# Writing out TensorE's order for the second mixer of a two-block transformer kernel

## The chip, the cores and the metric

The kernel runs on one core of a Trainium2 chip. The metric is the device time of one execution in microseconds (us). The profile is of one execution and its span is counted from the first instruction to the last. TensorE is PE in the profile (PEld is its weight load), VectorE is DVE, ScalarE is ACT, GpSimd is POOL, and SP is the queue that issues most DMAs.

## The reference, cut to what matters

Two blocks run one after the other on 512 tokens of width 1024: a first block (feed-forward, a mixer of three attention branches, feed-forward) and a second block. In the second block a mixer precedes a convolved feed-forward layer. Only the second mixer is changed. It computes:

```
h = rms_norm(x, pre_mix_norm);  proj = h @ w_in            # 1024 -> 6688 columns
q, k, v = split(silu(causal_dwconv(q|k|v)))                # delta rule: 8 heads of 128
o_a = gdn_chunked(l2(q)/sqrt(128), l2(k), v, g, beta)      # scan over chunks, one triangular solve each
o_a = rms_norm(o_a, gdn_norm_w) * silu(z_a)
x_s, b, c = split(silu(causal_dwconv(x_s|b|c)))            # state space: 16 heads of 64, 2 groups
y = (ssd_chunked(x_s, dt, a, b, c) + d * x_s) * silu(z_s)
o_s = rms_norm(y, per group)
x = x + rms_norm(concat(o_a, o_s) @ w_out, post_mix_norm)
```

## The kernel before, in words

Activations lie with features on the partitions and the 512 tokens along the free axis. A large product is made in **steps**: one step multiplies a 128x128 tile of weights with a 128x512 tile of activations as three matmuls (`mm3`, lines 163 to 169), since weights and activations are split in a high and a low half. `wload` (line 146) fetches 4 x 256 columns of weights (512 KB, two buffers) by SP and makes the two halves: ACT casts the high one (line 157), VectorE, or POOL where `k.lo` is set, subtracts for the low one (line 158). One such load serves 8 steps. `gemm_steps` (line 179) is a generator that yields after each step and calls `evac` when a 128-column result is complete; `gemm_fm` runs it to its end. The results of a group of 256 columns use two of three PSUM banks (tag g); small matmuls and transposes use tags a (1 bank), b (3) and r (1).

`Mix2.run` (line 1794) calls the parts in order: `gates` (line 1369: step sizes, decays and their cumulative sums); `gdn_k` and `gdn_a` for both halves of the heads (convolved keys, their transposes, norms, and the tables A = k k^T times decay, line 1504); `gdn_qv`, `blocks32` (line 1538: POOL inverts the 32x32 diagonal blocks of all tables, between DMAs through DRAM), `gdn_qe`, `gdn_qk` (scores); `inverses` (line 1574: the blocks are joined to the inverses of 128x128 tables); `gdn_scan` (line 1615: a serial chain over four chunks); `gdn_norm` (line 1656, with the turning back of the outputs, line 1672); `ssd_gemms`, `ssd` (line 1704), `gdn_z`, `ssd_z` (gates), `ssd_norm`; the product with w_out over 16 tiles, `os` and `oa`, of which `oa` (the delta rule) comes first in the sum; and the closing norm, whose factor is spread over partitions by TensorE and multiplied in before the feed-forward layer.

`conv_silu` (line 1289) evacuates a product with conv: a VectorE product (line 1293), an ACT scaling (1294), three VectorE multiply-adds (1296) and the ACT silu (1298 or 1300). `turned` (line 1337) makes four transposes into one bank. `row` (line 1344) broadcasts a row of decays by one matmul into bank r.

The order of each engine's instructions comes from the framework's scheduler, which goes by the order of the program as priority and by its own model of times. Two things steer it: `high_priority` around the weight halves, and `after=` (line 161), which ties the start of a product behind a matmul of the scans. Only the first mixer has TensorE's order written by hand (line 848, `manual_schedule`): there TensorE runs its instructions in the order of the program text, while the other engines are scheduled as everywhere.

Of the kernel before, what the change touches and what calls it, by code (L numbers as in the profile page):

```python
# [4 lines left out]

# [22 lines left out]
class K:  # L28
# [150 lines left out]
    def gemm_steps(self, w, c0, ncols, x, evac, kmax=4, after=None):  # L179

        nk = len(x)
# [1093 lines left out]
class Mix2:  # L1275
# [25 lines left out]

    def ztile(self):

        return self.k.sp.tile([128, 2, 512], F32, name=self.k.uid("zs"), tag="zs", bufs=2)
# [39 lines left out]
    def row(self, i=None, pick=None):  # L1344


        ps = self.k.ps("row", "r")
# [21 lines left out]
    def gates(self):  # L1369
# [7 lines left out]
        self.rt = k.norm_of(k.row_sums(k.sumsq(self.h)), D)  # L1377
        self.R = k.spread(self.rt)
        f = k.tmp("smf")
        nc.scalar.copy(f[:32], ps[:32])  # L1380
        pt = k.ps("smt")
# [14 lines left out]
        k.load_consts("cums")  # L1396
        pc = k.ps("pc")
# [29 lines left out]
        pt = k.ps("prow")  # L1427
# [5 lines left out]
        nc.vector.tensor_copy(self.pick, k.c("pick"))  # L1433

# [4 lines left out]
    def gdn_k(self, hf):  # L1439
        k, nc, a = self.k, self.nc, self.a  # L1440
        self.st[hf] = {"k": []}
# [7 lines left out]
        k.gemm_fm(a["w_in_2"][0], 1024 + hf * 512, 512, self.y, ev_k)  # L1449

    def gdn_qv(self, hf):
        k, nc, a = self.k, self.nc, self.a
        win = a["w_in_2"][0]
        st = self.st[hf]
        st["q"], st["v"] = qt, vb = self.big("q"), self.big("vb")

        def ev_q(m, ps):
            self.gconv(hf * 4 + m, ps, qt[:, m])

        def ev_v(m, ps):  # L1460
            t = k.tmp("vf", tag="f")
            self.gconv(16 + hf * 4 + m, ps, t)
            pt = self.turned(t, "a")
            for b in range(NB):
                nc.scalar.activation(vb[:, m, b * 128:(b + 1) * 128], pt[:, b * 128:(b + 1) * 128], AF.Copy,
                                     scale=self.vscale[:, b, hf * 4 + m:hf * 4 + m + 1])

        k.gemm_fm(win, hf * 512, 512, self.y, ev_q)
        k.gemm_fm(win, 2048 + hf * 512, 512, self.y, ev_v)

    def gdn_a(self, hf):
        k, nc = self.k, self.nc
        st = self.st[hf]
        ks = st["k"]

        (x, xv), (r, rv), (t, tv), (_, b2) = (self.per_head("kn" + c) for c in "xrtb")
        st["kd"] = []
        for m in range(4):

            pt, kd = self.turned(ks[m], "b"), k.tmp("kd", tag="kd")  # L1480
            self.sums_turned(xv[:, :, m:m + 1], pt)
            for b in range(NB):
                s = slice(b * 128, (b + 1) * 128)
                nc.scalar.activation(kd[:, s], pt[:, s], AF.Copy, scale=self.dec[:, b, hf * 4 + m:hf * 4 + m + 1])
            st["kd"].append(kd)
# [8 lines left out]
        for m in range(4):  # L1494
            hh = hf * 4 + m
# [3 lines left out]
            nc.scalar.activation(d1, d1, AF.Exp, scale=-1.0)  # L1499
            pkk = k.ps("pkk", "b")  # L1500
            for b in range(NB):
# [3 lines left out]
                                               op0=ALU.mult, op1=ALU.mult)  # L1505

    def gdn_qe(self, hf):

        k, nc = self.k, self.nc
        st = self.st[hf]  # L1510
        qt = st["q"]
        st["qe"] = qe = self.per_head("qe")[0]
        x, xv = self.per_head("qx")
        for m in range(4):
            self.sums_turned(xv[:, :, m:m + 1], self.turned(qt[:, m], "b"))
        nc.vector.tensor_scalar(qe, x, EPS, 128.0 * EPS, op0=ALU.add, op1=ALU.mult)

    def gdn_qk(self, hf):
        k, nc = self.k, self.nc
        st = self.st[hf]  # L1520
# [502 lines left out]
```

## Time and profile before

| | before |
|---|---|
| three runs, us | 2233.55, 2235.99, 2236.47 (median 2235.99) |
| profiled execution, us | 2238.18 (span 2236.5) |
| TensorE busy | 2173.7 us, 97% |
| VectorE, ACT, POOL busy | 1255.2 (56%), 933.8 (42%), 325.1 us (15%) |
| DMA | 202.39 MB, mean 90 GB/s |
| mean granted TensorE clock | 0.991 |

The second mixer runs from about 1308 to 1856 us of the span, the first from about 415 to 943. In the table of 40 slices each slice is 55.9 us; a digit 9 is nine tenths or more. Busy times of matmuls overlap, since they are pipelined: what one costs is read from the distance of starts, not from its own duration. A group of instructions has its idle time beside it, with what ended that time.

### The profile page before, as it was taken

The numbers are of one execution on the slowest core, as the hardware profiler recorded it, in microseconds if no ns is written. First come the engines' busy times: TensorE is split into PE (matmuls) and PEld (weight loads), VectorE is DVE, ScalarE is ACT, GpSimd is POOL, SyncE is SP. The second block draws the span as 40 slices with busy tenths as digits, with TensorE's granted clock in tenths as the row PEclk, the third lists the DMA queues.
The fourth block names the chain that finished last, engine by engine and source line by source line (L and its number), as shares of the span: only waits on it lengthen the run. The fifth ranks groups of instructions, "written<-read, shape, count | busy, mean of one in ns | idle before, by whom it ended". The sixth has DMA issues, their size and how long they took to land. (4 is left out here: it accounts for less than half of the span.)

```text
span 2236.5 us, 27895 instructions
## 1 busy us (share of the span) xinstructions
PE 2173.7 (97%) x10700; PEld 1759.4 (79%) x10700; DVE 1255.2 (56%) x2155; ACT 933.8 (42%) x1537; POOL 325.1 (15%) x340
## 2 busy tenths in 40 slices
PE   8999999999999999999999999999999898999998
PEld 6788888777677777788888877878777787888887
DVE  4544433575699654544343347866677526777623
ACT  4333322355555444332322237554556525444421
POOL 0110100011122222011110021550312100000000
PEclk9999999999999999999999999999999998999999
DMA  4233333322222223333333332331122223333332
GB/s 152 86 113 104 95 109 113 94 67 69 69 85 72 66 76 95 113 89 102 95 95 108 113 88 76 86 111 39 56 67 57 76 94 113 95 96 103 95 94 94
DMA packets 198508, 202.39 MB, mean 90 GB/s; under 512 B 19556, under 2 KB 184063, under 8 KB 198375
## 3 DMA queue, kind: packets, MB, share of 16 engines
q1 hardware_dynamic: 197607, 198.12, 29.8%
q0 software_dynamic: 768, 2.49, 0.4%
q8 instruction: 84, 1.38, 0.3%
q14 instruction: 49, 0.40, 0.1%
HBM read 192.70 MB, written 7.88 MB: 90 GB/s over the span
## 5 line engine op out<-in xcount | busy, mean ns | idle before, releaser
L163 PE MATMUL pg<-yh,whi 128*128 128x512 f32 x1856 | 745.6, 402 | 5.9 <-ACT yh L225 2.3
L169 PE MATMUL pg<-yh,wlo 128*128 128x512 f32 x1856 | 730.2, 394 | 1.2 <-DVE wlo L158 1.1
L168 PE MATMUL pg<-yl,whi 128*128 128x512 f32 x1856 | 729.7, 393 | 0.0
L158 DVE TENSOR_TENSOR wlo<-raw,whi 128x1024 fp32r<-128x1024 f32 x341 | 423.7, 1243 | 517.7 <-ACT whi L157 513.7
L157 ACT CAST whi<-raw 128x1024 fp32r<-128x1024 f32 x349 | 362.1, 1038 | 633.2 <-PE pg L168 429.7
L163 PEld LDWEIGHTS pg<-yh,whi 128*128 128x128 f32 x1856 | 350.3, 189 | 81.7 <-issue 9.1
L169 PEld LDWEIGHTS pg<-yh,wlo 128*128 128x128 f32 x1856 | 349.9, 189 | 75.4 <-DVE wlo L158 2.9
L168 PEld LDWEIGHTS pg<-yl,whi 128*128 128x128 f32 x1856 | 350.3, 189 | 67.5 <-issue 2.5
L163 PE MATMUL pg<-hidh,whi 128*128 128x512 f32 x352 | 138.7, 394 | 0.0
L169 PE MATMUL pg<-hidh,wlo 128*128 128x512 f32 x352 | 138.0, 392 | 0.0
L168 PE MATMUL pg<-hidl,whi 128*128 128x512 f32 x352 | 136.6, 388 | 0.0
L361 POOL TENSOR_TENSOR hp<-ut,sg 128x512 f32<-128x512 f32 x44 | 73.3, 1667 | 424.1 <-DVE ut L359 399.5
L217 ACT CAST hidh<-hp 128x512 fp32r<-128x512 f32 x44 | 27.3, 620 | 142.5 <-POOL hp L361 142.3
L169 PEld LDWEIGHTS pg<-hidh,wlo 128*128 128x128 f32 x352 | 66.1, 188 | 15.5
L1910 DVE SCALAR_TENSOR_TENSOR fo<-ft,fcw,fo 128x511 f32<-128x511 f32 x88 | 65.8, 749 | 21.7 <-ACT fo L1907 20.5
L168 PEld LDWEIGHTS pg<-hidl,whi 128*128 128x128 f32 x352 | 66.1, 188 | 14.8
L163 PEld LDWEIGHTS pg<-hidh,whi 128*128 128x128 f32 x352 | 66.2, 188 | 13.1
L218 DVE TENSOR_TENSOR hidl<-hp,hidh 128x512 fp32r<-128x512 f32 x44 | 30.4, 691 | 79.6 <-ACT hidh L217 79.6
L715 POOL TENSOR_SCALAR s<-s,den 128x256 f32<-128x256 f32 (+3 forms) x80 | 42.5, 533 | 190.6 <-DVE den L714 180.0
L1951 PE MATMUL pd<-whi,hidh 128*128 128x512 f32 x176 | 69.4, 394 | 0.0
L1952 PE MATMUL pd<-whi,hidl 128*128 128x512 f32 x176 | 69.4, 394 | 0.0
L1953 PE MATMUL pd<-wlo,hidh 128*128 128x512 f32 x176 | 69.2, 396 | 0.0
(502 smaller groups left out, 3000.1 us busy)
## 6 DMA issues: line engine op xcount, KB each, us to landing
raw<-in_w_in SPq DMA_DIRECT2D x100, 512.0 KB
raw<-in_ffn_w_gate SPq DMA_DIRECT2D x40, 512.0 KB
raw<-in_ffn_w_up SPq DMA_DIRECT2D x40, 512.0 KB
raw<-in_ffn_w_down SPq DMA_DIRECT2D x40, 512.0 KB
raw<-in_w_up SPq DMA_DIRECT2D x40, 512.0 KB
raw<-in_w_out SPq DMA_DIRECT2D x24, 512.0 KB
raw<-in_w_down SPq DMA_DIRECT2D x22, 512.0 KB
raw<-in_w_branch SPq DMA_DIRECT2D x12, 512.0 KB
```

Source lines behind the costliest of these rows:

```text
L157: nc.scalar.copy(hi, raw)
L158: (self.lo or nc.vector).tensor_sub(lo, raw, hi.bitcast(F32))
L163: first = mm(out, whi, xhi, start=start, stop=False)
L168: mm(out, whi, xlo, start=False, stop=False)
L169: mm(out, wlo, xhi, start=False, stop=stop)
L218: nc.vector.tensor_sub(lo, x, hi.bitcast(F32))
L361: nc.gpsimd.tensor_mul(p, ut, sg[m])
L715: nc.gpsimd.tensor_scalar(p[:, :w], p[:, :w], den, 1.0, op0=ALU.mult, op1=ALU.mult)
L1910: nc.vector.scalar_tensor_tensor(o[:, s:], t[:, :T - s], k.fcw[:, j:j + 1], o[:, s:], op0=ALU.mult, op1=ALU.add)
L1951: nc.tensor.matmul(pss[b], xh[:, s], hi[:, i], start=st, stop=False)
L1952: nc.tensor.matmul(pss[b], xl[:, s], hi[:, i], start=False, stop=False)
L1953: nc.tensor.matmul(pss[b], xh[:, s], lo[:, i], start=False, stop=sp)
```

## The change

TensorE's order in the second mixer is written out by hand. A generator `products()` makes the 544 product steps of the mixer one after the other; `fill(n)` takes n of them, and `later(n, do)` puts small work behind the n-th step from now. Because a conv's result is handed over in the call of its last step, `later(10, ...)` leaves 9 steps between (k), 11 leaves 10 (q) and 9 leaves 8 (v and x).

- The parts become generators that yield where product steps go. `gates` stops at steps 3, 6, 13 and 24; the inverses of both halves begin at step 184 with one step between sections; each scan has 3, 3 and 1 steps between its hand-offs, and its outputs (p3) come behind the state update (p4). The eight outputs of the delta rule are turned from 16 steps (first half) and 26 steps (second half) behind the second scan; the state-space groups begin at step 298; the last state-space gate ends at step 416; each state-space norm is summed 8 and spread 11 calls after its last gate.
- Keys are transposed one by one behind their conv (`gdn_kt`), tables follow in pairs of `decay` and `table`, `blocks32` follows the last table.
- `row` uses banks r and a in turn. POOL makes the low weight halves in `gdn_z(0)` and `ssd_gemms(0)` too (12 loads), beside those of the keys as before. `load_consts("cums")` moves ahead of the products.
- The order of the sum of w_out is kept, but tiles are exchanged: the outputs of the delta rule are split into the slots that the state-space outputs had, ahead of step 416, and those of the state space into the slots of the normed input.
- While the closing norm is computed, TensorE makes 7 and 8 matmuls of 128x512 whose results are not used.

The core of the diff:

```
+    def later(self, n, do):
+        at = self.done + n
+        i = sum(d[0] <= at for d in self.due)
+        self.due.insert(i, (at, do))
...
     def row(self, i=None, pick=None):
-        ps = self.k.ps("row", "r")
+        self.nrow += 1
+        ps = self.k.ps("row", "ra"[self.nrow % 2])
...
+    def idle(self, n, a, b):
+        k = self.k
+        ps = k.ps("idle", "r")
+        for _ in range(n):
+            self.nc.tensor.matmul(ps, a[0][:, :128], b[0], start=True, stop=True)
...
         def ev_v(m, ps):
             t = k.tmp("vf", tag="f")
             self.gconv(16 + hf * 4 + m, ps, t)
-            pt = self.turned(t, "a")
+            self.later(9, lambda: turn(m, t))
...
+        def products():
+            k.lo = nc.gpsimd
+            yield from self.gdn_k(0)
+            yield from self.gdn_k(1)
+            k.lo = None
+            yield from self.gdn_q(0)
+            yield from self.gdn_v(0)
+            yield from self.gdn_q(1)
+            yield from self.gdn_v(1)
+            k.lo = nc.gpsimd
+            yield from self.gdn_z(0)
+            yield from self.ssd_gemms(0)
+            k.lo = None
+            yield from self.ssd_gemms(1)
+            yield from self.gdn_z(1)
+            yield from self.ssd_z()
+            yield from k.gemm_steps(a["w_out_2"][0], 0, D, self.out, ev, nk=16)
...
+        def fill(n):
+            for _ in range(n):
+                next(work, None)
+                self.done += 1
+                while self.due and self.due[0][0] <= self.done:
+                    self.due.pop(0)[1]()
...
+        with self.tc.manual_schedule(engines={mybir.EngineType.PE}):
+            gates = self.gates()
+            next(gates)
+            for n in (3, 6, 13, 24):
+                upto(n)
+                next(gates)
+            upto(184)
+            both = [self.inverses(hf) for hf in range(2)]
+            for _ in range(7):
+                for steps in both:
+                    next(steps, None)
+                    fill(1)
+            woven(self.gdn_scan(0))
+            for m in range(4):
+                self.gdn_qk(1, m, 5 * m)
+            fill(19)
+            woven(self.gdn_scan(1))
+            for hf in range(2):
+                self.gdn_norm(hf)
+                for m in range(4):
+                    self.later(16 + 10 * hf + 2 * m, partial(self.gdn_out, hf, m))
+            upto(298)
+            group = self.ssd()
+            for g in range(2):
+                woven(group(g))
...
+            self.out += [k.split(self.st[hf]["q"][:, m], "oa", slot) for hf in range(2) for m in range(4)]
+            upto(416)
+            self.out += [k.split(x, "os", k.yslot) for x in self.xs[:4]]
+            upto(544)
+            idle = lambda n: self.idle(n, self.out[0], self.out[8])
+            sums = k.row_sums(sq)
+            idle(7)
+            pb = k.spread(k.norm_of(sums, D), copy=False)
+            idle(8)
```

## Rows read from the trace of the kernel before

**Rows 1.** Stretches: start:end, length, busy us (instructions) by engine, granted clock, DMA

```profile
core 0: us, PE busy (x) PEld busy (x) DVE busy (x) ACT busy (x) POOL busy (x), PEclk, DMA share, GB/s
1308.00:1856.00 548.00, 522.44 (x2998) 420.69 (x2998) 361.17 (x626) 289.32 (x534) 140.46 (x138) 0.98 0.27 79
425.00:890.00 465.00, 453.41 (x2353) 356.07 (x2352) 315.67 (x793) 236.92 (x462) 94.56 (x138) 0.99 0.25 74
1478.70:1482.10 3.40, 3.40 (x11) 2.71 (x10) 1.25 (x3) 2.51 (x6) 2.16 (x3) 0.50 0.52 189
1768.10:1772.30 4.20, 4.17 (x10) 3.30 (x11) 1.23 (x1) 1.04 (x1) 0.00 (x0) 0.50 0.00 0
1855.80:1861.00 5.20, 5.20 (x12) 4.09 (x13) 5.20 (x9) 3.43 (x6) 0.00 (x0) 0.50 0.59 189
...
1788.00:1828.00 40.00, 40.00 (x177) 32.85 (x176) 11.42 (x11) 12.41 (x16) 0.00 (x0) 1.00 0.29 93
```

**Rows 2.** TensorE's waits, 1308 to 1856 us: total us, times, longest

```profile
PE pg L168 <- DVE oal L218: 4.7, 1, 4.7
PE pb L321 <- POOL ry L244: 3.8, 4, 1.7
PE tr L1341 <- POOL q L1670: 3.2, 5, 1.5
PE tr L1341 <- ACT vf L1298: 2.6, 2, 2.4
PE pg L163 <- ACT yh L225: 2.3, 1, 2.3
PE tr L1341 <- ACT kf L1298: 1.9, 1, 1.9
PE pc L1400 <- DMA ct<-in_consts: 1.6, 1, 1.6
PE pkk L1503 <- DVE A L1504: 1.3, 1, 1.3
PE prow L1429 <- DVE parts L1426: 1.0, 1, 1.0
```

**Rows 3.** Order of time, two convs (k, then v): first and last operation of each

```profile
1341.29 0.69 DVE L1293 TENSOR_TENSOR cx<-pg,R 128x512 f32<-128x512 f32 x1 [2.90 <-PE pg L169]
...
1349.27 0.63 ACT L1298 ACTIVATE kf<-kf 128x512 f32<-128x512 f32 x1
...
1414.12 0.69 DVE L1293 TENSOR_TENSOR cx<-pg,R 128x512 f32<-128x512 f32 x1
...
1419.62 0.63 ACT L1298 ACTIVATE vf<-vf 128x512 f32<-128x512 f32 x1 [1.79 <-DVE vf L1296]
```

**Rows 4.** Order of time, behind the second scan: last copy, first four POOL products

```profile
1582.45 0.57 ACT L1654 COPY q<-sc 128x512 f32<-128x512 f32 x1
...
1590.51 5.61 POOL L1670 TENSOR_TENSOR q<-q,onr 128x512 f32<-128x512 f32 x4 [27.56 <-ACT whi L157]
```

**Rows 5.** Order of time, gates: the small transposes and the log decays

```profile
1318.46 0.43 PE L1383 MATMUL smt<-ct_base,smf 32*128 32x32 f32 x4
...
1328.39 0.25 DVE L1394 TENSOR_TENSOR g<-dt,nega 128x96 f32<-128x96 f32 x1
```

**Rows 6.** Order of time: last table, last write-backs of the blocks, a turned tile

```profile
1405.48 0.35 DVE L1504 SCALAR_TENSOR_TENSOR A<-pkk,knb,d 128x128 f32<-128x128 f32 x1
...
1480.78 3.13 POOL L1569 DMA_DIRECT2D A<-xtscr  x4 [0.39 <-DMA xtscr<-zs]
...
1491.36 0.60 PE L1341 MATMUL tr<-ct_base,vf 128*128 128x128 f32 x4
```

**Rows 7.** A stretch in the first state-space group (columns as in rows 1)

```profile
1628.00:1668.00 40.00, 39.56 (x190) 30.12 (x188) 31.34 (x47) 22.00 (x30) 4.51 (x4) 1.00 0.23 67
```

**Rows 8.** POOL's weight splits, one VectorE operation beside one, its shape elsewhere

```profile
L158 POOL TENSOR_TENSOR wlo<-raw,whi 128x1024 fp32r<-128x1024 f32 x8 | 19.7, 2467 | 31.2 <-ACT whi L157 31.1
...
1331.31 2.26 DVE L1296 SCALAR_TENSOR_TENSOR kf<-cx,gcw,kf 128x509 f32<-128x509 f32 x1
...
L1296 DVE SCALAR_TENSOR_TENSOR bc<-cx,scw,bc 128x509 f32<-128x509 f32 x4 | 3.0, 744 | 0.0
```

More of the change, by code (lines that the diff above doesn't have):

```diff
@@ L4 @@
 from contextlib import ExitStack
+from functools import partial
 import numpy as np
@@ L1447, in ev_k, with gdn_kt @@
             ks.append(t)
[L1449 to L1462, printed above, removed]
-            pt = self.turned(t, "a")
[L1464 to L1471, printed above, removed]
+            self.later(10, lambda: self.gdn_kt(hf, m))
+        yield from k.gemm_steps(a["w_in_2"][0], 1024 + hf * 512, 512, self.y, ev_k)
+    def gdn_kt(self, hf, m):
         k, nc = self.k, self.nc
         st = self.st[hf]
[L1474 to L1485, printed above, removed]
+        (x, xv), (r, rv), (t, tv), (_, b2) = st["n"]
+        pt, kd = self.turned(st["k"][m], "b"), k.tmp("kd", tag="kd")
+        self.sums_turned(xv[:, :, m:m + 1], pt)
+        for b in range(NB):
+            s = slice(b * 128, (b + 1) * 128)
+            nc.scalar.activation(kd[:, s], pt[:, s], AF.Copy, scale=self.dec[:, b, hf * 4 + m:hf * 4 + m + 1])
+        st["kd"].append(kd)
+        if m < 3:
+            return
         nc.vector.tensor_scalar(x, x, EPS, None, op0=ALU.add)
@@ L1690, in ev_x, with turn @@
             self.conv_silu(ps, *cols(m), t)
+            self.later(9, lambda: turn(m, t))
+        def turn(m, t):
             pt = self.turned(t, "a")
@@ L1707, in ssd, with group @@
         free = self.slots()
-        for g in range(2):
+        def group(g):
             bm, cm = self.bc[g], self.bc[2 + g]
@@ L1719, in ssd @@
             bt = next(free)
+            yield 1
             nc.scalar.copy(bt, self.turned(bm, "b"))
@@ new lines, in table @@
+            def table(c, p):
+                L = k.tmp("L")
+                self.decay_t(L, 8 + 2 * (g * 4 + c) + p)
+                nc.vector.tensor_mul(L, L, cb)
+                return L
+            ls = []
+            for c in range(5):
+                new = []
+                for p in range(2):
+                    if c < 4:
+                        new.append(table(c, p))
+                        yield 2
+                if c:
+                    m = g * 4 + c - 1
+                    pd = k.ps("pyd", "b")
+                    for p, L in enumerate(ls):
+                        for b in range(NB):
+                            nc.tensor.matmul(pd[p * 64:(p + 1) * 64, blk[b]],
+                                             self.xdt[g][:, c - 1, b * 128 + p * 64:b * 128 + p * 64 + 64], L[:, blk[b]],
+                                             start=True, stop=True)
+                    po = k.ps("pyo", "b")
+                    for b in range(1, NB):
+                        nc.tensor.matmul(po[:, blk[b]], states[b][:, (c - 1) * 128:c * 128], cm[:, blk[b]],
+                                         start=True, stop=True)
+                    er = self.row(pick=pick[:, (c - 1) * 128:c * 128])
+                    x = self.xs[m]
+                    nc.vector.tensor_add(x, x, pd)
+                    t = k.tmp("yo")
+                    nc.scalar.copy(t[:, 128:], po[:, 128:])
+                    nc.vector.tensor_mul(t[:, 128:], t[:, 128:], er[:, 128:])
+                    nc.vector.tensor_add(x[:, 128:], x[:, 128:], t[:, 128:])
+                    yield 4
+                ls = new
@@ L1764, in ssd_z @@
+        return group
     def ssd_z(self):
@@ new lines, in run, with upto, woven, slot @@
+        work = products()
+        def fill(n):
[4 more added lines that the diff above has]
+                    self.due.pop(0)[1]()
+        def upto(n):
+            fill(n - self.done)
+        def woven(steps):
+            for n in steps:
+                fill(n)
+        with self.tc.manual_schedule(engines={mybir.EngineType.PE}):
[17 more added lines that the diff above has]
+                self.gdn_norm(hf)
+                for m in range(4):
+                    self.later(16 + 10 * hf + 2 * m, partial(self.gdn_out, hf, m))
[3 more added lines that the diff above has]
+                woven(group(g))
+            free, tags = self.slots(F32R), iter(("A", "QK", "A", "kd") * 4)
+            def slot(s):
+                tag = next(tags)
+                return next(free) if tag == "A" else k.tmp(s, F32R, tag)
+            self.out += [k.split(self.st[hf]["q"][:, m], "oa", slot) for hf in range(2) for m in range(4)]
[7 more added lines that the diff above has]
+            idle(8)
```

219 lines of the change are left out of this document (109 added, 110 removed).

## The prediction

> **What bounds it now.** I read the table of 40 slices first (TensorE at nine tenths or more in nearly every slice), then the stretches, TensorE's waits in the second mixer, and the instructions in order of time around each wait. TensorE is the bound: of the 548 us of the second mixer it is busy 522.4, so 25.6 us of waits are all that an order of its own work can return there directly [rows 1]. What it must do is not changed: a product step is three 128x512 matmuls, 177 of them in 40.0 us, so 0.68 us a step and 544 steps in the mixer [rows 1]. Nine pairs of waiter and releaser make 22.4 of the 25.6 us; the smaller ones hold 3.2 [rows 2]. Beside the waits stands the granted clock: three stretches at 0.50, TensorE's lower level of 1.2 GHz, each behind one of the longer waits, in which 11, 10 and 12 matmuls take 3.4, 4.2 and 5.2 us [rows 1]. At the full rate they take half, so 1.7, 2.1 and 2.6 us are lost.
>
> The first mixer already has its TensorE order written out. There 11.6 us of 465 are waits, 2.5%, against 4.7% here [rows 1]. By that share the second mixer would keep 13.7 us.
>
> **The parts, against the profiled execution (2238.2 us, its span 2236.5).** Minus is faster. VectorE, ScalarE and POOL keep their orders from the scheduler; TensorE now stops at whatever is late.
>
> *Output projection, -6.4.* The gated outputs of the delta rule come first in the sum over 16, split 40 steps earlier. This takes away the wait for their low halves, 4.7 us, and half of the 2.1 us that is left of the waits for the norms' rows once the closing one (1.7) is taken off; the other half I give to the gates [rows 2]. With it goes the slow stretch behind, 2.1 [rows 1]. New: each state-space norm is read 7 steps (4.8 us) after its last gated output. The nearest chain of as many operations, a conv's, takes 6.1 us [rows 3], so 1.3 us each is the bound and nothing the other; I take 1.5 for both. The split that moves is DVE and ACT work at a time when both wait for TensorE. The loads of weights keep their order on SP.
>
> *Closing norm, -2.6.* The chain from the last product to the next stage stays, 0.6, 1.7 and 2.3 us of waits in it; the first is among the smaller ones [rows 2]. Fifteen extra 128x512 matmuls (3.4 us by the step) lie inside these waits, so they cost nothing; were the clock at its lower level they would take 6.8, which is 2.2 over the 4.6 and the bound on that side. What they may return is the slow stretch after the wait, 2.6 [rows 1]. I take all of it, since the longest idle piece left is then under a microsecond.
>
> *Turning the delta rule's output, -1.7.* It returns 3.2 us [rows 2]. Now the first four turns come 16 steps (10.9 us) after the second scan; in the trace 13.1 us pass from the end of the last copy to the end of the first four POOL products [rows 4]. Two other turns lie between (0.5 each): 1.2 short, and 0.3 for the second four. Bounds -3.2, and +1.7 if two of POOL's moved splits (below, 2.5 each) come first.
>
> *Turns behind the convs of v and x, -2.2.* It returns 2.6 and 0.7 of the smaller waits [rows 2] and a slow stretch of 1.7 [rows 1]. Each turn now stands 8 steps (5.4 us) behind its last product. The conv takes 6.1 us from first to last operation in one case and 8.6 in another [rows 3]. The channels come in pairs; of 8 pairs half have other small work between. Four pairs at 0.7 make 2.8, at 3.2 they make 12.8. I take 2.8: the nearest row is a v conv, while the 8.6 has POOL's split beside it. Bounds -2.2 and +7.8.
>
> *Turns behind the convs of k, +0.2.* It returns 1.9 and 1.3 [rows 2]. Nine steps (6.1 us) against 6.1 to 8.6: two uncovered pairs at nothing or 2.5; here the row of 8.6 is the k one, so 1.7 each. Bounds -3.2 and +1.8. Queries have 10 steps: nothing.
>
> *Gates, +3.0.* It returns 1.6 (the cumulative-sum constants, now loaded ahead of the first weights on SP), 1.0 and 1.05 [rows 2]. But the cumulative sums stand 7 steps behind the small transposes, and from these to the log decays 10.2 us pass, a chain of small dependent VectorE operations with one foreign operation of 0.7 in it [rows 5]. So 9.5, less 4.8 of steps and 0.4 of the transposes: 4.3 to 5.0 us of waiting, I take 4.5, all queued work on TensorE behind it. The nearest wait, 4.7, had a slow stretch that cost 2.1 [rows 1, 2]; I add that. Bounds 0.7 and 3.5.
>
> *Blocks and inverses, +1.0.* The 32x32 inversion on POOL runs from the last table to the last of four issues that write back, 78.1 us [rows 6]. From that table (step 88) to the first inverse (step 184) lie 96 steps, 65.3 us, 13 turned tiles at 0.5 [rows 6], four sets of scores (estimated as two turns, 1.1) and eight single rows (0.3): 78.6. The landing comes on top. Its DMAs on SP stand behind weight loads as before. I take 1.0; bounds 0 and 8. The scans' hand-offs get three steps (2.0 us) each: nothing.
>
> *State-space groups, +1.0.* VectorE is busy 31.3 of 40 us in the first group [rows 7]. Four convs of some 2.9 us now fall into its 39 steps (44 us with its own matmuls): 34 and 12 against 44 leaves 2 late, less 0.7 of small waits gone, rounded. Bounds -0.7 and +6.
>
> *Moved splits, 0.* Twelve weight splits go from VectorE to POOL, 2.47 us each [rows 8], one per 8 steps (5.4 us); nothing on the path as long as POOL isn't held.
>
> The sum is -7.7: 2230.5 for this execution, and the median of the runs stands 2.2 under it, so **2228 us**.
>
> **Rivals.** *As good as the first mixer:* 25.6 less 13.7 and 4.7 of clock returned, -16.6, **2219 us**. For it: the same kind of order there. Against it: the wait in the gates alone is a third of 13.7.
>
> *Waits change places:* the convs of v and x at half their upper bound (+5) and the groups at +3 eat the sum: **2236 us**, no change. For it: VectorE is at 78% where work is added.
>
> *Slower, by the shared port:* during a POOL split one 128x509 VectorE operation took 2.26 us, where the same shape takes 0.74 elsewhere [rows 8]. The twelve splits move to just the steps in which the scans hand over through VectorE, with some 0.3 us of slack. If each delays one hand-off by 1.5 us, 1.2 come through, 14 in all, and the time is **2242 us**; it decides once some 10 of the 12 hit one (12.2 us). Against it: VectorE itself is spared the twelve splits, and most hand-offs last under a microsecond.
>
> The Trainium skill, "SBUF — State Buffer", section "SBUF: two separate sides", says that a VectorE operation with two SBUF inputs and a GpSimd operation that reads SBUF exclude each other for the whole instruction. Where each split met such an operation at its start, 2.47 us would be lost each time and this rival would read 2254. The trace has one such case at 1.5 us and no row of a whole 2.47.
>
> **How the numbers follow.** What a measurement of this kernel can tell from no change is about 0.2%, 4.5 us. My forecast has 0.42 (own range 2222 to 2233, of it 0.05 above 2231.5), the first mixer's share 0.22, the exchanged waits 0.18 (of them 0.15 within 4.5 us, 0.03 above), the port 0.18. Faster 0.37 and 0.22, so 0.59; the same 0.20; slower 0.21. The range runs from 2213, a little under the best rival, to the port's 2242; more than that needs several upper bounds at once.
>
> **What would show it.** Right: no wait over 1 us at the start of the output projection; full clock after the closing norm; a wait of 4 to 5 us before the cumulative sums, with a slow stretch; small waits of about 1 us at the turns. Wrong: the sums start at once (then the chain was not what I read), the inverses wait for the DMA of the blocks, VectorE operations of over 2 us beside POOL splits in the scans, or TensorE's waits in the mixer under 14 us or over 30.

## The result and the profile after

The kernel became slower: 2295.36 us (median of four runs, 2290.75 to 2297.43) against 2235.70 before, a ratio of 1.0262 with a 95% interval of 1.0249 to 1.0275. The forecast was 2228, with a range that ended at 2242. The profiled execution has a span of 2295.7 us against 2236.5, and TensorE is busy 2198.4 us of it, 96%.

The lines of the changed file stand 1 to 131 further down: `conv_silu` is at 1290 to 1301, the turns at 1348, the rows at 1358, the sums of the gates at 1412, the tables of the keys at 1515 (product) and 1516 (multiplication).

Stretches of the kernel after, in the columns of [rows 1]: the whole mixer; from the start of step 44 to the start of step 100 (counted in the order of time), which holds the multiplications of all eight key tables in both kernels; and a plain product stretch near the end.

```profile
core 0: us, PE busy (x) PEld busy (x) DVE busy (x) ACT busy (x) POOL busy (x), PEclk, DMA share, GB/s
1305.00:1917.00 612.00, 550.11 (x3010) 446.24 (x3011) 357.24 (x613) 297.70 (x540) 167.68 (x150) 0.94 0.24 70
1360.30:1462.30 102.00, 77.16 (x286) 60.31 (x284) 55.88 (x132) 48.83 (x109) 3.38 (x3) 0.78 0.16 42
...
1838.00:1909.00 71.00, 71.00 (x313) 58.37 (x312) 19.81 (x19) 21.61 (x27) 0.00 (x0) 1.00 0.31 96
```

And the same steps of the kernel before:

```profile
1356.50:1408.00 51.50, 50.16 (x254) 40.62 (x253) 46.13 (x119) 35.19 (x94) 3.14 (x2) 1.00 0.27 75
```

The mixer grew from 548 to 612 us (the whole span grew by 59: this execution is 3 us shorter ahead of the mixer and 2 behind it). Idle TensorE time went from 25.6 to 61.9 (612 less 550.1), so 36 of the 64 us are waits. The other 28 are busy time: 5 for the fifteen extra matmuls, and for the rest the clock, whose mean fell from 0.98 to 0.94 (0.04 of 612 us is an estimate of 24). And 50 us of the 64 lie in one place: steps 44 to 99 take 102 us in place of 51.5, at a mean clock of 0.78. The plain product stretch at the end is as fast as before (71 us at 1.00).

TensorE's waits in the mixer, to be held against [rows 2]:

```profile
engine line waited for: us in total, times, longest us
PE pkk L1515 <- DVE A L1516: 23.4, 24, 3.7
PE tr L1348 <- ACT vf L1299: 6.8, 3, 3.9
PE pc L1412 <- DVE g L1406: 6.4, 1, 6.4
PE tr L1348 <- ACT xs L1301: 6.1, 3, 4.3
PE tr L1348 <- ACT kf L1299: 4.8, 3, 2.5
PE pn L289 <- DVE sq L274: 3.7, 2, 2.3
PE row L1358 <- DVE xdt L1755: 2.9, 2, 2.7
PE tr L1348 <- DVE L L1367: 2.4, 1, 2.4
```

The first line is new in size: before, this pair of waiter and releaser was one wait of 1.3 us. The order of time shows what it is; a part of the first table in the kernel after:

```profile
1366.31 0.35 DVE L1516 SCALAR_TENSOR_TENSOR A<-pkk,knb,d 128x128 f32<-128x128 f32 x1
1366.71 0.76 PE L1515 MATMUL pkk<-kf 128*128 128x128 f32 x2 [3.73 <-DVE A L1516]
...
1367.51 0.35 DVE L1516 SCALAR_TENSOR_TENSOR A<-pkk,knb,d 128x128 f32<-128x128 f32 x1 [0.86 <-PE pkk L1515]
1367.92 0.80 PE L1515 MATMUL pkk<-kf 128*128 128x128 f32 x2 [0.44 <-DVE A L1516]
1368.75 0.35 DVE L1516 SCALAR_TENSOR_TENSOR A<-pkk,knb,d 128x128 f32<-128x128 f32 x1 [0.89 <-PE pkk L1515]
```

A table is a loop over four blocks: a product of 128x128, then the multiplication that reads it. All four blocks share one PSUM bank, and each product waits until the multiplication of the block before has ended: 0.8 us for a product, 0.4 for the multiplication, and again, with a longer wait behind the first block, whose decays aren't ready. Of the 23.4 us, the eight waits behind a first block make 15.8 and the sixteen others 7.6, so two thirds are a late input that the loop lets TensorE run into. All products and multiplications of the tables in the kernel before (durations are least, median and longest, then first and last start):

```profile
L1503 PE MATMUL pkk<-kf x64: 270/275/377, 1355.0 to 1405.2; 128*128 128x128 f32 x64
L1504 DVE SCALAR_TENSOR_TENSOR A<-pkk,knb,d x32: 334/344/354, 1366.9 to 1405.5; 128x128 f32<-128x128 f32 x32
```

and in the kernel after:

```profile
L1515 PE MATMUL pkk<-kf x64: 270/377/583, 1362.6 to 1449.5; 128*128 128x128 f32 x64
L1516 DVE SCALAR_TENSOR_TENSOR A<-pkk,knb,d x32: 343/351/352, 1366.3 to 1449.9; 128x128 f32<-128x128 f32 x32
```

Before, the first products started 12 us ahead of the first multiplication: the scheduler had put the first blocks of three tables (one in each bank b) among product steps, and wove the later blocks of several tables with one another and with steps. In the order of time:

```profile
1355.03 0.49 PE L1503 MATMUL pkk<-kf 128*128 128x128 f32 x2
...
1357.21 0.39 PE L1503 MATMUL pkk<-kf 128*128 128x128 f32 x2
...
1359.17 0.49 PE L1503 MATMUL pkk<-kf 128*128 128x128 f32 x2
```

After, the first product is 4 us ahead, and nothing stands between the four blocks of a table.

The Trainium skill, "PSUM — Partial Sum Buffer", section "PSUM bank collisions raise a hardware error", says that two engines must not touch one bank in the same partitions at once, whichever columns they use, and that the compiler's scheduler makes one wait for the other. By that rule turn-taking is to be expected wherever a text alternates the two; the trace agrees, with 24 waits of 23.4 us, three for each of the eight tables.

### The profile page after: what moved, and what is told of

It reads as the page before. It is cut to its first block, busy times and chain, and to the rows that moved or that the text cites. A ratio compares the mean times of both kernels' runs of the same rounds, so it can differ in the third digit from the quotient of the medians.

```text
span 2295.7 us, 27885 instructions
## 1 busy us (share of the span) xinstructions
PE 2198.4 (96%) x10715; PEld 1782.1 (78%) x10715; DVE 1251.5 (55%) x2143; ACT 942.4 (41%) x1543; POOL 352.4 (15%) x352
## 4 chain that ended last, share of the span: by engine, by line
PE 82%; DVE 9%; ACT 4%; issue 2%; POOL 1%; DMA 0%; SPq 0%; POOLq 0%; DVEq 0%; ACTq 0%
PE pg L164 22%; PE pg L170 22%; PE pg L169 22%; PE pd L2084 2%; PE pd L2082 2%; PE pd L2083 2%; DVE wlo L159 1%; ACT whi L158 1%; PE po L722 1%; PE pt L704 1%; DVE kf L1297 1%; DVE xs L1297 1%; PE pkk L1515 1%; DVE q L1297 1%; DVE cx L1294 1%
## 5 line engine op out<-in xcount | busy, mean ns | idle before, releaser
L164 PE MATMUL pg<-yh,whi 128*128 128x512 f32 x1856 | 760.2, 410 | 3.8 <-ACT qk L745 2.0
L159 DVE TENSOR_TENSOR wlo<-raw,whi 128x1024 fp32r<-128x1024 f32 x329 | 406.6, 1236 | 507.0 <-ACT whi L158 503.4
```

The lines of the kernel that those rows point to most:

```text
L159: (self.lo or nc.vector).tensor_sub(lo, raw, hi.bitcast(F32))
L164: first = mm(out, whi, xhi, start=start, stop=False)
```

## Experiments

Each was compared with runs of the kernel before on the same chip (2235.7 to 2237.3 in the median). The sums below go by the medians; single differences under about 4 us are read as no clear change. Runs on different chips are set side by side by these medians.

### 1. The four products of a table first

```
             for b in range(NB):
                 s = slice(b * 128, (b + 1) * 128)
                 nc.tensor.matmul(pkk[:, s], ks[m][:, s], ks[m][:, s], start=True, stop=True)
+            for b in range(NB):
+                s = slice(b * 128, (b + 1) * 128)
                 nc.vector.scalar_tensor_tensor(st["A"][:, m * NB + b], pkk[:, s], b2[:, b, m:m + 1], d1[:, s],
```

> In each of the eight tables of the keys the four products are issued first and the four multiplications behind them, instead of one by one in turn. Theory A (the turn-taking: TensorE, now held to the order of the text, waits for each multiplication before the next 128x128 product, 24 waits of 23.4 us, and falls to half clock between them; steps 44 to 89 take 90.6 us against 40.9 before, of which 23.5 are waits and some 26 the clock): TensorE has no wait for A, steps 44 to 89 take 43 to 50 us, and the time falls by 40 to 48 us, to about 2250. Rival B (VectorE and ScalarE are late with the decays, 15.8 of the 23.4 us stand ahead of the first multiplication of a table, and with three banks the wait only moves to the next user of a bank): waits of 12 us or more stay in these steps, and the time falls by less than 20, to 2277 or more. Rival C (the time is lost in the other parts): within 5 us of 2295.

Measured: 2260.96 us, ratio 1.0112 (1.0095 to 1.0129), 34 us less. Steps 44 to 99 in this kernel:

```profile
1361.40:1427.80 66.40, 58.31 (x285) 48.24 (x284) 52.09 (x132) 47.93 (x108) 3.41 (x3) 0.92 0.24 64
```

One whole table in its order of time:

```profile
1363.71 1.05 PE L1515 MATMUL pkk<-kf 128*128 128x128 f32 x8
```

A table is one piece of 1.05 us. The stretch is 36 us shorter, and the waits for A went from 23.4 to 2.1 us: theory A's mechanism, though its 40 to 48 us were too much. Other waits grew: for turns of k from 4.8 to 6.8 us, of q from 2.0 to 3.2, and one of 2.5 us for the bank of a table came up at the scores. So the tables hold over half of the loss, and 25 us stand elsewhere.

### 2. The kernel before with the same loop

```
                 nc.tensor.matmul(pkk[:, s], ks[m][:, s], ks[m][:, s], start=True, stop=True)
+            for b in range(NB):
+                s = slice(b * 128, (b + 1) * 128)
                 nc.vector.scalar_tensor_tensor(st["A"][:, m * NB + b], pkk[:, s], b2[:, b, m:m + 1], d1[:, s],
```

> The kernel before, with the four products of each key table issued ahead of the four multiplications. Theory A (there the scheduler had set product steps between the four, so that the turn-taking cost one wait of 1.3 us): between 3 us faster and 2 slower than the kernel before. Rival (the turn-taking costs in any order): 6 us or more faster.

Measured: 2232.94 us, ratio 0.9987 (0.9978 to 0.9996), 3 us less: just past theory A's bound, half of what the rival needed, and by itself hardly clear of no change. The same turn-taking costs at most some 3 us under the scheduler's order and 34 under the written one: the order is what made it dear.

### 3. One product step between the four blocks

```
-        self.later(n + 2, table)
+        for b in range(NB):
+            self.later(n + 2 + b, partial(table, b))
```

> The changed kernel with the four products of a table of the keys one product step apart, each multiplication still right behind its product. Theory A (TensorE needs other work between a product and the multiplication that it waits for, as the scheduler had put it): close to the run with the four products first, 2250 to 2268. Rival B (VectorE and ScalarE are late with the decays, and TensorE waits for the first multiplication of a table all the same): 2280 or more, with waits of 15 us or more for A.

Measured: 2280.95 us, ratio 1.0201 (1.0152 to 1.0249). Neither came out: 12.2 us of waits for the tables are left, between the two, in six waits of up to 5.5 us, so one step between the blocks takes away the turns but not the late decays. The size stays open: two runs took 2269.5 and 2271.5 us at a mean clock of 0.988, two 2290.4 and 2291.0 at 0.977 and 0.976. The profile is of the longest, and in it the clock is at half for 44 us over the inverses:

```profile
PE p L1638 <- DMA A<-xtscr: 1.1, 1, 1.1
...
1516.70:1561.10 44.40, 44.40 (x429) 34.54 (x428) 14.15 (x18) 9.01 (x17) 6.39 (x8) 0.50 0.08 25
```

Half of 44 us is near the 20 us between the pairs; whether the shorter runs were free of it, no profile shows (see 5).

### 4. The gates seven steps later

```
-            for n in (3, 6, 13, 24):
+            for n in (3, 6, 20, 31):
```

> Only the stops of the gates are moved: the cumulative sums from step 13 to 20, the rows from 24 to 31. Theory A (each wait is its own, worth its length and the slow clock behind it): the 6.4 us ahead of the sums fall under 2 and the slow stretch behind goes, 6 to 8 us less, 2288. Rival B (the chain of gates ends no earlier, so the turned keys and the tables, which need the sums, wait longer by what is saved): within 2 us of 2295.

Measured: 2296.19 us, ratio 1.0269 (1.0252 to 1.0285): no change. Rival B. The sums were moved by 4.8 us and still waited 4.3 us, since the chain of gates ended later; its last operation in the order of time, first of the changed kernel:

```profile
1328.39 0.26 DVE L1406 TENSOR_TENSOR g<-dt,nega 128x96 f32<-128x96 f32 x1
```

and of this one:

```profile
1331.68 0.26 DVE L1406 TENSOR_TENSOR g<-dt,nega 128x96 f32<-128x96 f32 x1
```

While TensorE goes on with product steps, a second conv of a key arrives on VectorE and its first operation stands among the small ones of the chain, one of which also took 2.42 us beside a split on POOL. And a turn of a key, some 20 us later, waited 4.7 us in place of 2.5 at the same point. The 4.8 us of steps took only 2.1 us off the wait: on an engine that gets work with each step, a distance of steps buys less than its length.

### 5. The turns four steps later

```
-            self.later(10, lambda: self.gdn_kt(hf, m))
+            self.later(14, lambda: self.gdn_kt(hf, m))
...
-            self.later(11, lambda: norm(m))
+            self.later(15, lambda: norm(m))
...
-            self.later(9, lambda: turn(m, t))
+            self.later(13, lambda: turn(m, t))
...
-            upto(298)
+            upto(304)
```

> On the kernel with the four products first (2261): the turns of keys, queries, values and state-space inputs come four steps later (2.7 us), and the state-space groups start six steps later, since they need the last turn. Theory A (each turn stands too few steps behind its conv; the waits for convs are 22.2 us there, with some 10 of the 17 us that the clock takes): 12 to 22 us less, 2239 to 2249. Rival E (VectorE and ScalarE are behind in these stretches, so that the waits move to the tables, the scores or the inverses): less than 5 us, 2256 or more.

Measured: 2276.55 us, ratio 1.0181 (1.0166 to 1.0196), 16 us more than in 1. Theory A missed. The time is in rival E's range, and the waits did move to the inverses, but not for its reason: TensorE waits there for POOL's chain and its DMA, not for VectorE or ScalarE. The turns' waits went nearly all. The first of TensorE's waits in this kernel is now:

```profile
PE p L1636 <- DMA A<-xtscr: 14.9, 2, 13.6
```

The stretch around it:

```profile
1480.00:1542.00 62.00, 49.12 (x499) 38.71 (x500) 14.15 (x18) 11.29 (x23) 18.30 (x22) 0.50 0.15 50
```

And POOL's last write-backs of the blocks, in the order of time:

```profile
1487.84 3.13 POOL L1619 DMA_DIRECT2D A<-xtscr  x4 [0.46 <-DMA xtscr<-zs]
```

The last table was done at 1409.9 and the inverses started at 1491.6, 82 us later: POOL's chain, which [rows 6] put at 78.1 us without the landing of its data. In the changed kernel TensorE reached the inverses 89 us after the last table, too late to wait. Worse than the 14.9 us is what follows: half clock from 1480 to 1542. The same inverses in the changed kernel, with only waits of 0.4 and 1.3 us for turns in the 13 us ahead of them, ran at full clock:

```profile
1539.00:1567.00 28.00, 28.00 (x500) 22.15 (x499) 14.24 (x18) 11.21 (x22) 8.65 (x8) 1.00 0.15 40
```

So about the same 500 matmuls, most of them of 32x32, took 49 us of busy time in place of 28: this wait, at the start of the inverses, cost 21 us on top of itself. The clock, once down, came back only about when they had ended. In experiment 3 the same came behind waits of 0.8 and 1.1 us; why there and not in the changed kernel stays open.

### 6. The same, inverses at step 204

```
-            upto(184)
+            upto(204)
```

> On the kernel with later turns (2276.6): the inverses start at step 204 instead of 184, one number changed. Theory G (with the early waits gone TensorE reaches the inverses before POOL's chain of the 32x32 blocks, 82 us from the last table, has ended: 14.9 us of waits on its DMA, and 61.4 us of half clock behind them, in which about 46 us of work lose 23): both go, and the time is 2233 to 2245. Rival H (the half clock belongs to the small matmuls of the inverses, whatever stands before them): the waits go but a stretch of 40 us or more at half clock stays, 2258 to 2266. Rival E (VectorE and ScalarE are behind): the waits turn up in the scans or the groups, 2265 or more.

Measured: 2261.53 us, ratio 1.0117 (1.0099 to 1.0136), 15 us less. The wait for the DMA went, and the half clock shrank from 61 to 10 us; the inverses ran at 1.00 (27 us). So theory G holds for the clock, and H doesn't, though the time lies in H's range: it missed G's 2245 by 16 because other waits had come up. The two largest of this kernel:

```profile
PE tr L1348 <- DVE L L1367: 9.2, 3, 5.3
PE pg L170 <- POOL wlo L159: 9.1, 1, 9.1
```

The second of them in the order of time:

```profile
1493.34 1.56 POOL L1622 DMA_DIRECT2D X<-xscr  x2
1494.92 4.67 POOL L159 TENSOR_TENSOR wlo<-raw,whi 128x1024 fp32r<-128x1024 f32 x2
...
1497.33 0.79 PE L170 MATMUL pg<-yh,wlo 128*128 128x512 f32 x1 [9.09 <-POOL wlo L159]
```

A weight split that the change moved to POOL stands behind the chain of blocks in POOL's queue, and TensorE waits for it. With the inverses early, the product steps that need this split came after the chain.

### 7. Gates, groups and norms moved as well

```
-            for n in (3, 6, 13, 24):
+            for n in (2, 5, 21, 32):
...
-            upto(304)
+            upto(308)
...
-        self.later(8, sums)
-        self.later(11, scaled)
+        self.later(11, sums)
+        self.later(14, scaled)
```

> On the kernel of the first run of this set: gates at steps 2, 5, 21 and 32, the state-space groups at 308 instead of 304, each state-space norm three steps later. Theory A (each wait that is left, 6.4 in the gates, 3 to 5 in the groups, 6.5 at the norms, is worth its length and the slow stretch behind it): 8 to 15 us under that run, about 2226. Rival (as with the gates alone, what is waited for comes later by what is saved): within 3 us of that run.

Measured: 2248.66 us, ratio 1.0061 (1.0045 to 1.0078), 13 us less, as theory A had it for the difference. The 9.1 us on POOL stayed.

### 8. The twelve splits back on VectorE

```
-            k.lo = nc.gpsimd
             yield from self.gdn_z(0)
             yield from self.ssd_gemms(0)
-            k.lo = None
...
-            upto(204)
+            upto(208)
```

First in the changed kernel itself (the splits alone), then on top of 7 (both).

> The twelve low weight halves of the first gate and the first state-space group are made by VectorE again, not by POOL. Rival P (the shared port: VectorE operations beside a POOL split take 1 to 2.4 us in place of 0.2 to 0.7, and this is what holds the turns of the state-space inputs, 4.3 us, and the scans): 5 us or more faster, 2290 or less. Theory A (the port costs single operations and the waits come from VectorE's queue, in which the split itself is 1.24 us): between 2 us faster and 3 slower.

> On the kernel with gates, groups and norms moved (2248.7): the twelve weight splits of the first gate and the first state-space group go back to VectorE, and the inverses start at step 208. Theory I (in that kernel TensorE waits 9.1 us for a split that stands on POOL behind the chain of blocks, and 10.2 us of half clock follow): both go, 12 to 16 us less, 2232 to 2237, level with the kernel before. Rival E (VectorE, with twelve splits of 1.24 us more, is late for the scans and the groups): 2243 or more.

Measured: 2295.82 us (1.0249 to 1.0286) alone, no change, theory A; 2238.40 us, ratio 1.0013 (1.0003 to 1.0022) on top of 7, 10 us less. Theory I, a little smaller: the wait of 9.1 us is gone, and so is the half clock of 10.2 us behind it. The second edit also starts the inverses four steps later, but TensorE waits at the inverses in neither kernel, so the 10 us are put down to the splits (argued, not run apart). They are worth nothing in one kernel and about 10 us in the other: in the changed kernel they were hidden, since TensorE came to them after POOL's chain had ended.

### 9. Bank a, the second scan's outputs, and the groups again

The rows back in one bank, on the kernel of 1, and the turned inputs in banks b, on top of 8:

```
-        ps = self.k.ps("row", "ra"[self.nrow % 2])
+        ps = self.k.ps("row", "r")
```

```
-            pt = self.turned(t, "a")
+            pt = self.turned(t, "b")
             nc.vector.tensor_mul(self.xdt[g][:, m % 4].rearrange("p (b h d) -> p b h d", b=NB, h=2),
```

> On the kernel with the four products first (2261): the broadcast rows use bank r alone again, not r and a in turn. Theory A (in the state-space groups the rows and the turned inputs now hold bank a against each other: 2.9 us of rows waiting for the turned input's reader, 2.5 us of the turn waiting for a row's reader, each with a slow stretch): 5 to 8 us less, 2253 to 2256. Rival F (rows two steps apart need two banks): new waits of rows for the reader of the row before, so no gain or up to 6 us slower, 2259 to 2267.

> On the first run of this set: the state-space inputs are turned into one of the three banks b, not into bank a, which the rows now use in turn with r. Theory A (rows and turned inputs hold bank a against each other, 4 to 5 us with a slow stretch of 1.7): 4 to 7 us less than that run. Rival F (the three banks b are then the ones waited for, or the inputs are late anyhow): within 2 us of it, or slower.

The first: 2263.10 us (1.0103 to 1.0137), no change; the rows waited for one another, as rival F had it (3.4 us and three waits of 1.1). The second: 2233.53 us, ratio 0.9989 (0.9979 to 0.9998), 5 us less, theory A: the waits on bank a (2.0 and 3.5 us) went, and less came up in their place (2.0 us for a table; those for POOL's products rose from 5.3 to 6.8).

On top of the second, later outputs of the delta rule, and then later groups:

```
-                    self.later(16 + 10 * hf + 2 * m, partial(self.gdn_out, hf, m))
+                    self.later(27 + 10 * hf + 2 * m, partial(self.gdn_out, hf, m))
...
-        self.later(14, scaled)
+        self.later(14 if g else 17, scaled)
```

```
-            upto(308)
+            upto(320)
```

> On the best kernel of the written order (2233.5): the delta rule's outputs are turned from 27 steps behind the second scan instead of 16, and the first state-space norm is spread three steps later. Theory A (waits and the half clock behind them still add up: 6.8 us for POOL's products, 2.1 for the norm, some 5 of clock): 8 to 14 us less, 2220 to 2226. Rival E (VectorE is the bound of the stretch from the second scan to the second group, 100 us in which it takes on convs, turned inputs and tables; TensorE then waits in the groups instead): 2230 or more.

> On the best kernel of the written order (2231.0): the state-space groups start at step 320 instead of 308. Theory A (a backlog of VectorE, whose convs, norms and turned inputs fall together there): most of the 11 us of waits and 1.7 to 3.4 us of clock go, 5 to 10 us less, 2221 to 2226. Rival E (VectorE is the bound of the whole stretch, so that the waits come up in the second group or at the norms): 2228 or more.

Measured: 2231.03 us, ratio 0.9977 (0.9968 to 0.9985), and 2227.61 us, ratio 0.9965 (0.9951 to 0.9978): 2.5 and 3.4 us less, each too small to be clear by itself, 6 together, and each less than theory A had. The first is rival E's; the second lies between the two, nearest to rival E. In the first, TensorE's waits of 6.8 us behind the second scan went, and others in the first group took their place, the largest for VectorE's tables (TensorE's waits in it):

```profile
PE pyd L1828 <- DVE L L1813: 4.7, 1, 4.7
PE pc L1412 <- DVE g L1406: 3.1, 1, 3.1
PE tr L1348 <- ACT kf L1299: 2.8, 2, 2.3
PE row L1358 <- DVE L L1367: 2.4, 2, 1.2
```

The last kernel is the fastest of all, 8.6 us under the kernel before in the same set of runs. Its mixer, as one stretch:

```profile
1305.00:1845.00 540.00, 520.21 (x3006) 427.11 (x3006) 363.57 (x623) 290.49 (x536) 141.74 (x138) 0.98 0.27 79
```

### 10. The changed text in the scheduler's order

```
-        with self.tc.manual_schedule(engines={mybir.EngineType.PE}):
+        if True:
```

> The changed program with TensorE's order left to the scheduler, as in the kernel before: only the bracket that holds TensorE to the text is taken away; the text, the exchanged slots, the splits on POOL and the extra matmuls stay. Theory A (the loss is the written order, which puts small work at a fixed distance of steps before its chain is done, so that TensorE stops): within 10 us of the kernel before, 2226 to 2247. Rival D (the loss lies in the other parts: keys turned one by one, 40 loads of ScalarE's function tables in place of 34, splits on POOL, exchanged slots): 2270 or more.

> On the changed program in the scheduler's order (2261.7): the inverses stand at step 204 of the text instead of 184. Theory G (all that this order loses against the kernel before is the wait for the blocks, 11.5 us, and the 54.6 us of half clock behind it, about 24 us): 2222 to 2232, level with the kernel before or a little faster. Rival D (the exchanged slots, splits on POOL and keys turned one by one cost time of their own): 2240 or more.

> The same two edits on the changed text in the scheduler's order (2245.6). Theory I: its wait of 8.0 us for a split on POOL and the half clock behind it go, and half of the 8.2 us for POOL's products ahead of the groups: 2228 to 2234, a little under the kernel before, since exchanged slots and closing norm are left. Rival D (the other parts of the changed text cost time of their own): 2240 or more.

> The changed text in the scheduler's order with the splits back on VectorE (2232.4): the turned state-space inputs in banks b, the delta rule's outputs eleven steps later in the text. Theory A: its wait of 7.6 us of a turned input for bank a and the 10.2 us of half clock behind it go, 9 to 13 us less, 2219 to 2224; then the written order adds nothing to the same edits in the scheduler's order. Rival E: 2229 or more.

The second takes the inverses to step 204, the third the splits to VectorE and the inverses to 208, the fourth the turned inputs to banks b and the outputs to `later(27 + ...)`. Measured, one upon the other: 2261.67 (1.0099 to 1.0129), 2245.57 (1.0028 to 1.0064), 2232.41 (0.9975 to 0.9994) and 2233.65 us (0.9983 to 1.0002). The first missed both theories: freed of the written order the text loses the waits for the tables, but TensorE then waits 11.5 us for the blocks, with the clock at half for 54.6 us. The wait, by TensorE's waits of the first of these kernels:

```profile
PE p L1634 <- DMA A<-xtscr: 11.5, 2, 10.0
```

and the stretch:

```profile
1482.00:1542.00 60.00, 48.52 (x498) 37.79 (x497) 14.15 (x18) 10.82 (x22) 17.23 (x18) 0.54 0.16 51
```

The inverses at 204 took back 16 us, which is short of theory G and in rival D's range, for a wait of 8.0 us for a split on POOL came up; the splits, with the inverses at 208, took 13 more, as theory I had it. So the scheduler's order of this text had the same two faults, both set by the text. The last edit, for a wait of 7.6 us, gave nothing (rival E): one of 5.7 us of the rows took its place. Both orders end close together, 2227.6 written and 2232.4 scheduled, but the written one had some edits more, and the fully mended text was not run in the scheduler's order. Nor is much left to the rest of the change: in the set of the 2227.6, the kernel before with nothing but its table loop turned round (experiment 2) took 2232.9. So whether writing out the order gains anything by itself stays open.

### 11. The closing norm without the extra matmuls

```
-            idle(7)
...
-            idle(8)
```

> The fifteen matmuls whose results are not used are left out of the closing norm. As the prediction had it: the slow stretch behind the norm comes back, 2 to 3 us slower, 2298. Rival (they hold the chain as long as they save, since a slow stretch stands behind them in this kernel too): within 1 us of 2295.

Measured: 2298.38 us, ratio 1.0277 (1.0257 to 1.0297), against 1.0262 (1.0249 to 1.0275) with them. The 3.0 us agree with the prediction, but the intervals overlap, so it isn't settled. In the profile without them the waits of 1.7 and 2.3 us are back, and the clock is at 0.69 over 11 us in place of 0.84 (the kernel after, then this one):

```profile
1909.00:1920.00 11.00, 10.23 (x48) 8.25 (x47) 6.50 (x12) 4.32 (x7) 1.01 (x1) 0.84 0.71 232
...
1913.00:1924.00 11.00, 6.38 (x25) 4.92 (x25) 8.28 (x15) 5.18 (x10) 1.01 (x1) 0.69 0.62 215
```

## Why the prediction was wrong

**The step that failed** stands in "Turns behind the convs of k": "It returns 1.9 and 1.3 [rows 2]". The 1.3 is the wait of a table product for a multiplication. It was booked as a wait that a written order takes away, and the tables had no term of their own. The trace of before showed the opposite: the wait was small because the scheduler had woven the blocks of several tables with one another and with product steps. The diff says what becomes of that: `table` issues all four blocks behind one step. It cost 34 us (experiment 1), over half of the 67 us between forecast and measurement. That the order made the cost, and not the loop by itself, is shown by experiment 2 (3 us) and by the changed text in the scheduler's order, where no wait for A is among the longer ones (experiment 10). Of the prediction's own signs of being wrong two came: waits of over 30 us, here 61.9, and VectorE operations of over 2 us beside POOL splits in the scans (2.6 and 2.4 us in the second), though without these splits the time was the same (experiment 8, alone).

**Gates, +3.0:** the mechanism was right, the size too small. The wait was 6.4, not 4.5, and 6.8 us at half clock lay over its end. The chain took 11.7 us, not 10.2: four operations of a key's conv stand in it where one of 0.7 stood before. And the 10.2 us held more than was read in them: one of the small operations, 0.26 us elsewhere, took 2.33 beside a POOL split, in the kernel before:

```profile
1324.36 2.33 DVE L258 SCALAR_TENSOR_TENSOR spe<-spe,spd 128x96 f32<-128x96 f32 x1
```

More distance took 2.1 us off the wait and nothing off the time (experiment 4).

**Turns, -2.2 for v and x, +0.2 for k, nothing for q:** wrong in sign for v and x, where 12.9 us of waits stand against 2.8: less the 3.3 returned this is +9.6, past the upper bound of 7.8; too small for k and q. The waits were 6.8 and 6.1 us for v and x, 4.8 for k, 2.0 for q. Four pairs at 0.7 were the term; but by the measure of [rows 3] convs of v now take 5.1 to 8.0 us and those of x 5.4 to 12.6, against the 5.4 that eight steps cover. They had not grown: in the kernel before it was 5.9 to 7.9 and 6.2 to 12.2, so all eight stood in the trace. One row of v and one of k were too thin a base.

**Output projection, -6.4:** right. Its first 24 steps take 21.9 us against 27.0, 5.0 less, and from step 380 to step 440, which hold both norms in both kernels, it is 51.1 against 58.2, 7.1 less. The wait of 4.7 for the low halves is gone; the two norms' waits came to 3.7 us where I had 1.5, and one of them (2.3) stands at the start of the projection, where none over 1 us was expected.

**Turning the delta rule's output, -1.7:** no wait there in the changed kernel; but with the other waits gone it came back as 6.8 us (experiment 9). Its upper bound of 1.7 was still too low. The kernel before also has a slow stretch here that the working left out (1594.8 to 1598.2 us at 0.50).

**Closing norm, -2.6:** consistent with 3.0, not settled. The extra matmuls took 5.2 us, not 3.4: 3.4 us of this stretch are still at half clock (1912.9 to 1916.3).

**Blocks and inverses, +1.0:** nothing in the changed kernel, and 14.9 us of waits with 21 of clock once TensorE was on time (experiment 5). Both the missing landing and what the slow clock does to the inverses lay outside the bound of 8.

**State-space groups, +1.0:** 5.3 us of waits on bank a, which the change had given to the rows too. The banks were not in the working.

**Moved splits, 0:** "nothing on the path as long as POOL isn't held". It is held, by the chain of blocks, for 82 us; about 10 us, hidden at first (experiment 8).

**The rivals:** "waits change places" was the nearest, but for the size. The shared port was not the cause (experiment 8, alone), though its working counted one VectorE operation drawn out beside a POOL split in the trace of before, where there are five, by 1.5 to 2.2 us each (one in the last section). And "as good as the first mixer" was not reached; the mended order idles about 20 us of 540 (540 less 520.2), 3.7% against 2.5%.

What of the last 25 us belongs to which part stays open: the edits were made on top of one another, and some showed a price only when another wait was gone.

## To carry to other kernels

When an order that a scheduler wove is written out by hand, look for every loop in the text in which two engines take turns on one PSUM bank: what was hidden by the weaving stands bare. Here each turn cost TensorE 0.4 us or more, the first of a table up to 3.7 for an input that was late, and a clock that fell. Issue all products first, then all that read them. Try first what this alone gives in the scheduled kernel: here it gave 3 us, the written order with all its edits 8.6. And after a wait has been mended, look again at the next fixed chain of another engine (here POOL's 82 us) before moving more work onto that engine.

## What the chip showed that was not expected

The half clock can last much longer than the 3.4 to 5.2 us stretches of [rows 1]: 61 us behind a wait of 14.9, while TensorE worked through the inverses' small matmuls, and 44 and 55 us in two others, behind waits of 1.1 and 11.5 (experiments 3 and 10). Behind a wait of 9.1 us that ended 12 us ahead of the inverses, it lasted 10.2 us, and they ran at full clock (experiment 6).

VectorE's smallest operations can lose a whole POOL instruction. In the kernel after, in the order of time:

```profile
1657.88 2.39 POOL L159 TENSOR_TENSOR wlo<-raw,whi 128x1024 fp32r<-128x1024 f32 x1 [4.91 <-ACT whi L158]
1657.96 2.33 DVE L237 SCALAR_TENSOR_TENSOR ont<-ont,onx 128x16 f32<-128x16 f32 x1
...
1660.42 0.17 DVE L237 SCALAR_TENSOR_TENSOR ont<-ont,onx 128x16 f32<-128x16 f32 x1
```

An operation of 0.17 us took 2.33, until the split had ended. The kernel before already had it:

```profile
1362.69 2.45 POOL L158 TENSOR_TENSOR wlo<-raw,whi 128x1024 fp32r<-128x1024 f32 x1 [5.50 <-ACT whi L157]
...
1362.78 2.39 DVE L236 SCALAR_TENSOR_TENSOR knt<-knt,knx 128x16 f32<-128x16 f32 x1
```

The Trainium skill, "SBUF — State Buffer", section "SBUF: two separate sides", says that such a pair exclude each other for the whole instruction; the trace agrees, 2.33 us in place of 0.17. The run without these splits showed no gain all the same (experiment 8, alone).
